# A chunked mLSTM encoder on one core: the forward state products move to other accumulator banks, and a token tile's norm joins the heads' norm

## The chip, the core and the metric

The kernel runs on one core of a Trainium2 chip. TensorE (PE in the profile) multiplies matrices into accumulator banks, VectorE (DVE) and ScalarE (ACT) work element by element and empty those banks, GpSimd (POOL) works on ordinary on-chip memory and issues some DMAs, SyncE (SP) issues most DMAs. Each engine goes through its own list of instructions in order and waits on semaphores for the others. The metric is the device time of one execution in microseconds (us).

## The reference, cut to what matters

The reference is one encoder layer on 2048 tokens of width 1024. It has an mLSTM mixer with four heads, run once forward and once backward over the tokens, a squared-ReLU MLP, and a gated embedding branch.

```python
def step(carry, xs):                       # one chunk of 128 tokens, all heads
    C, n, m = carry
    ...
    s = jnp.einsum('bhtd,bhsd->bhts', q_, k_) * d
    num = jnp.einsum('bhts,bhsv->bhtv', s, v_) + inter[..., None] * jnp.einsum('bhtd,bhvd->bhtv', q_, C)
    ...
    h = num / jnp.maximum(jnp.abs(den), jnp.exp(-m_t))[..., None]
    ...
    C = decay[..., None, None] * C + jnp.einsum('bhsv,bhsd->bhvd', w[..., None] * v_, k_)
...
h = (h_fwd + h_bwd)
h = h * lax.rsqrt(jnp.mean(jnp.square(h), axis=-1, keepdims=True) + EPS)     # the heads' norm
...
h = h + mix
h = h + sqrelu_mlp(rmsnorm(h, norm_mlp[i]), w1, w2)                          # the token norm
```

The two norms in this text are the heads' norm, one scale for each token and head, and the token norm ahead of the MLP, one scale for each token.

## The kernel before, in words

**Stages.** The kernel first projects the tokens to queries, keys, values and gates, and runs the backward states, from the start to 560 us. Then comes the chunk loop, to about 930 us, which is what the change touches. After it come the MLP's two matrix products and the gated branch, to the end. Every product in float32 precision is three matmuls of rounded parts (`mm3`, L185): high by high, high by low, low by high.

**Who sets the order.** The program writes the steps down by hand, as strings of step names (`ORDER`, L1519; `ORDER_1` and `ORDER_X`, L1564 and L1565). A scheduler of the framework then decides, from its own cost model and with the program's order as priority, in which order each engine issues its instructions and which buffer of a tag a tile gets. So the order on an engine can differ from the string. All engine calls outside the queues go through one helper, so nearly all rows of the profile have the line L100, and the tile names tell them apart.

**Accumulator banks.** There are three kinds (L65 to L72): four general banks (`ps_mm`), three for transposes (`ps_tr`) and one for scores (`ps_s`).

**A turn of the chunk loop** (L1566) works on chunk c. TensorE's part, by the tile that it writes: `pn` is the numerator of one direction (`nums`, L1006; step n0 forward, n1 backward), four general banks one after the other, each emptied by ScalarE's copy into `nt`. `pu` is the state product of a head (`state_update`, L781; step s): heads 0 and 1 take transpose banks, heads 2 and 3 general ones; VectorE's `Cn` reads it and forms the new state, which ScalarE rounds to `Chi` and VectorE subtracts to `Clo`. `pth` are the eight transposes of the finished heads of the chunk before (`transposes`, L1051; step T), in two transpose banks, read by VectorE's `og`; then ScalarE's `hThi` and VectorE's `hTlo`. `pS` are the scores of the next chunk (step S), whose masks come from ScalarE's exponentials `mb` (step e). `pso` are the two halves of the output projection of the chunk before (`out`, L1064; steps o0 and o1); VectorE's `xt` adds the input and SP stores the tile to `h1_d`.

**The heads' norm.** `norm` (L1026, step m) forms the denominators `rd` on VectorE, scales `nt`, and has ScalarE square each head into `jk` with the sum into a column of `ssh`. `norm_end` (L1045, step me) calls `rstd` (L169) on four columns: one VectorE operation (`rsa`), two on ScalarE (`rsy`), four small ones on VectorE (`rst`, `rsy`), and ScalarE scales the heads into `jk`.

**The token norm of the first half** (`Tokens0.steps`, L1155) is worked on in the chunk loop, since the tokens of early chunks are done by then. With XC = 6 (L1561), eight tiles are spread over turns 6 to 14: in turn c, `load` (xl) reads tile c - 6 into `raw`, and at the turn's end `norm` (xn) squares it on ScalarE with its sum in a column of its own (`ss1`), calls `rstd` on that one column and has VectorE scale it into `xs`. In turn c + 1, `tr` (xt) transposes it (`pt`, two transpose banks), ScalarE copies it into `zt`, and SP stores it.

**Buffers.** Tiles of 4 KB a partition share two tags: H with 39 buffers (L74) and O with 7 (L78). `raw`, `og`, `xt` and `zt` are of O.

Of the kernel before, what the change touches and what calls it, by code (L numbers as in the profile page):

```python
# [10 lines left out]
AF = mybir.ActivationFunctionType  # L11
ALU = mybir.AluOpType
# [4 lines left out]
P = 128  # L17
S = 2048
D = 1024
KD = D // P  # L20
NC = S // P
H = 4
# [3 lines left out]
DVX = DV + 2  # L26
# [9 lines left out]
def hybrid_mlstm_kernel(  # L36
# [20 lines left out]
    x, p, out = x[0], p[0, 0], out[0]  # L57
# [10 lines left out]
    def ps_tr(name):  # L68
        return psm.tile([P, 512], F32, tag="tr", bufs=3, name=name)
# [4 lines left out]
    def Ht(name, shape, dt=F32):  # L74

        return sb.tile(shape, dt, tag="H", bufs=NH, name=name)

    def Ot(name, shape, dt=F32):  # L78

        return sb.tile(shape, dt, tag="O", bufs=NO, name=name)  # L80
# [5 lines left out]
    class Engine:  # L86


        def __init__(self, engine):
            self.engine, self.last, self.strict = engine, None, False  # L90
# [18 lines left out]
    V, A, G, TE, SP = Engine(nc.vector), Engine(nc.scalar), nc.gpsimd, Engine(nc.tensor), nc.sync  # L109


    rowc = {}
# [10 lines left out]
    def act(o_, i_, func, **kw):  # L123
        name = "sigmoid" if func == AF.Sigmoid else "exp_ln"
        if name == "exp_ln" and table["set"] != name:
            in_order(lambda: A.preload_act_table_set("natural_log_exp_and_others"))
        table["set"] = name
        in_order(lambda: A.activation(o_, i_, func, **kw))
# [40 lines left out]
    def rstd(ss, n):  # L169

        T = lambda nm: sb.tile([P, 8], F32, tag=nm, bufs=3, name=nm)[:, :n]
        a, y, t = T("rsa"), T("rsy"), T("rst")
        V.tensor_scalar_add(a, ss, EPS)
        act(y, a, AF.Ln)
        act(y, y, AF.Exp, scale=-0.5)
        V.tensor_tensor(t, a, y, op=ALU.mult)
        V.tensor_tensor(t, t, y, op=ALU.mult)
        V.tensor_scalar(t, t, -0.5, 1.5, op0=ALU.mult, op1=ALU.add)
        V.tensor_tensor(y, y, t, op=ALU.mult)
        return y  # L180

    def small(nm, bufs=3):
        return sb.tile([P, 8], F32, tag=nm, bufs=bufs, name=nm)

    def mm3(ps, lh, ll, rh, rl, first, last, **kw):  # L185
        TE.matmul(ps, lh, rh, start=first, stop=False, **kw)
        TE.matmul(ps, lh, rl, start=False, stop=False, **kw)
        TE.matmul(ps, ll, rh, start=False, stop=last, **kw)
# [58 lines left out]
    class Prep:  # L247
# [16 lines left out]
        def square(self, j):  # L264
            if j == 0:
                self.ss, self.xs = small("ss"), []
            xs = Ht("xs", [P, D])
            A.activation(xs, self.raw[j], AF.Square, scale=1.0 / 32.0, accum_out=self.ss[:, j:j + 1])
            self.xs.append(xs)

        def norm(self):
            for j in range(4):
                self.square(j)
            self.scale()
# [55 lines left out]
        def steps(self):  # L330
            return [self.dma, self.norm] + [lambda k=k: self.tr(k) for k in range(KD)]
# [415 lines left out]
    def cols(t, d, c):  # L747

        return t.rearrange("p (d h c) -> p d h c", d=2, h=H)[:, d, :, c]
# [31 lines left out]
    def state_update(C, wk, vx, d, c):  # L781

        Cn = Ht("Cn", [P, H, DVX])
        for h in range(H):
            pu = (ps_tr if (h % 2 if d == 1 else h < 2) else ps_mm)("pu")[:, :DVX]
            mm3(pu, wk[:, 0, h], wk[:, 1, h], vx[0][:, h], vx[1][:, h], True, True)
            i = d * 64 + h * NC + c
            if C is None:
                V.tensor_copy(Cn[:, h, :], pu)
            else:  # L790
                V.scalar_tensor_tensor(Cn[:, h, :], C[:, h, :], dcb[:, i:i + 1], pu, op0=ALU.mult, op1=ALU.add)
        return Cn
# [140 lines left out]
    class Chunk:  # L933
        Cf = Cs = None

        def __init__(self, c):
            self.c = c

# [87 lines left out]
        def norm(self):  # L1026

            c, nt = self.c, self.nt
            rd = small("rd")
            for d in range(2):  # L1030
                den = nt[d][:, :, DV]
                r = rd[:, d * H:(d + 1) * H]
                V.scalar_tensor_tensor(r, den, -1.0, den, op0=ALU.mult, op1=ALU.max)
                V.tensor_tensor(r, r, cols(ecol, d, c), op=ALU.max)
            V.reciprocal(rd, rd)
            ss = small("ssh")
            jk = Ht("jk", [P, H, DV])
            for h in range(H):
                a, b = nt[0][:, h, 0:DV], nt[1][:, h, 0:DV]
                A.activation(a, a, AF.Copy, scale=rd[:, h:h + 1])  # L1040
                V.scalar_tensor_tensor(a, b, rd[:, H + h:H + h + 1], a, op0=ALU.mult, op1=ALU.add)
                A.activation(jk[:, h], a, AF.Square, scale=1.0 / 16.0, accum_out=ss[:, h:h + 1])
            self.ss, self.hr = ss, jk

        def norm_end(self):  # L1045
            rh = rstd(self.ss[:, :H], H)
            jk, nt = self.hr, self.nt
            for h in range(H):
                A.activation(jk[:, h], nt[0][:, h, 0:DV], AF.Copy, scale=rh[:, h:h + 1])
# [100 lines left out]
    class Tokens0(Right1):  # L1150
# [4 lines left out]
        def steps(self, t):  # L1155
            s = {}

            def load():
                s["raw"] = Ot("raw", [P, D])
                SP.dma_start(s["raw"], h1_d[t])  # L1160

            def norm():
                xs, ss = Ht("xs", [P, D]), small("ss1")
                A.activation(xs, s["raw"], AF.Square, scale=1.0 / 32.0, accum_out=ss[:, 0:1])
                r = rstd(ss[:, :1], 1)
                V.scalar_tensor_tensor(xs, s["raw"], r[:, 0:1], rowc["mlp"], op0=ALU.mult, op1=ALU.mult)
                s["xs"] = xs

            def tr():
                z = Ot("zt", [P, KD, P])  # L1170
                for g4 in range(2):
                    pt = ps_tr("pt")
                    for i in range(4):
                        k = g4 * 4 + i
                        TE.transpose(pt[:, i * P:(i + 1) * P], s["xs"][:, k * P:(k + 1) * P], ident)
                    A.copy(z[:, g4 * 4:g4 * 4 + 4], pt.rearrange("p (k t) -> p k t", t=P))
                sl = slice((t % 4) * P, (t % 4 + 1) * P)
                SP.dma_start(x0_d[t // 4, :, :, sl].rearrange("k p t -> p k t"), z)
            return [load, norm, tr]

        def zload(self, nm):
            j, l = int(nm[1]) - 1, int(nm[2]) - 1
# [235 lines left out]
    o, q = jobs[0, "o"], jobs[0, "q"]  # L1418
# [35 lines left out]
    p1 = pa[1][1]  # L1454
# [17 lines left out]
    for n, pr in ((0, pa[0][0]), (2, pa[0][1])):  # L1472
        e = pr.early()
# [40 lines left out]
    for at, f in zip(slots, steps[8:]):  # L1514
        at.append(f)
    assert len(slots) == len(steps) - 8

    ch = [Chunk(c) for c in range(NC)]
    ORDER = "n0 d1 s e T S p1 q n1 d2 k w sl m v d o0 o1 me".split()  # L1519

    def step(c, nm):
# [11 lines left out]
        if n2:  # L1533
# [7 lines left out]
    tr = {"o6a": o[6].groups[0], "o6b": o[6].groups[1], "o7a": o[7].groups[0], "o7b": o[7].groups[1], "D": z.dma, "D1": z.dma1, "p0": z.pre, "v0": z.split_v,  # L1541
          "e0": z.exps, "S0": z.scores, "k0": z.wk_split, "w0": z.weights, "q0": z.q_split,
          "d_": ch[1].dma, "p_": ch[1].pre}
# [12 lines left out]
    def row_load(nm, src):  # L1556
        rowc[nm] = Ht(f"row_{nm}", [P, D])
        SP.dma_start(rowc[nm], src.partition_broadcast(P))


    XC = 6  # L1561
    tp = {c: x0.steps(c - XC) for c in range(XC, XC + 8)}
    tp[XC][0] = lambda f=tp[XC][0]: (row_load("mlp", norm_mlp[0]), f())
    ORDER_1 = "n0 d1 s e T c6 S n1 d2 k w c7 q sl m v d o0 o1 me".split()  # L1564
    ORDER_X = "n0 d1 s e T S p1 q n1 xt d2 k xl w sl m v d o0 o1 me xn".split()  # L1565
    for c in range(1, NC - 1):  # L1566
        for nm in ORDER_X if c in tp or c - 1 in tp else ORDER if c > 1 else ORDER_1:
            if nm == "xt":

                tp.get(c - 1, [lambda: None] * 3)[2]()  # L1570
            elif nm in ("xl", "xn"):
                tp.get(c, [lambda: None] * 3)[("xl", "xn").index(nm)]()
            elif nm in ("c6", "c7"):
                wo[int(nm[1])].prep()
            else:
                step(c, nm)()
    TAIL = "d2 W n1 Z1 Z3 T n0 Z2 Z4 o0 m me P1 X1 o1 P2 T15 U3 U1 X2 U2 X3".split()
    l = ch[NC - 1]
# [34 lines left out]
    for i in range(2, NF // 2):  # L1613
        e0, e1 = ENTER[i - 1], ENTER[i]
        if i >= NF // 2 - 2:
            e0, e1 = (35, 38) if i == NF // 2 - 2 else (38, 40)
        down[max(e0 - 1, 0)].side.append(pairs[i].dma)
        steps = pairs[i].preps()
        for j, f in enumerate(steps):
            down[e0 + j * (e1 - e0) // len(steps)].side.append(f)  # L1620
# [73 lines left out]
```

## Time and profile before

| | us |
|---|---|
| median of 3 runs | 2441.32 |
| lowest and highest | 2438.54, 2443.88 |
| the profiled execution's own time | 2440.1 |
| its span, first to last instruction | 2438.4 |
| mean granted TensorE clock, of full speed | 0.995 |

The difference of 1.7 us between the execution's time and its span lies around the instructions. Rows of the profile give a start and a duration in us, the engine, the line, the operation, the tile written, the tiles read, the shape and the count. A bracket at the end of a row is the idle time of that engine just before the row and what ended it. A row of waits gives who waited for whom, the total in us, the number of times and the longest. The idle time of an engine that nobody waits for costs nothing.

The chunk loop in the trace: the first `pu` of chunks 1 to 14 starts at 579.00, 604.64, 626.38, 647.03, 668.40, 689.13, 710.46, 735.23, 760.07, 782.32, 807.26, 829.76, 855.53 and 877.08 us.

### The profile page before, as it was taken

To read this page: it belongs to the slowest core of one execution; us is meant where nothing else is said; L and a number is where in the kernel's file an instruction comes from. 1 tells how busy PE (TensorE), PEld (TensorE's weight loads), DVE (VectorE), ACT (ScalarE), POOL (GpSimd) and SP (SyncE) were. 2 spreads that over 40 slices of the span, in tenths; PEclk is the share of its full clock that TensorE was granted. 3 is DMA by queue.
4 is the path that set the end of the run, shared out by engine and by line. 5 is a ranking of instruction groups with operands and counts; after the bars stand their busy time and mean duration, and the time that the engine had idled before them with its cause. 6 is when DMAs were issued, how large, how long until landed. Compare 5 with 4: busy or idle time off the path is not lost.

```text
span 2438.4 us, 31719 instructions
## 1 busy us (share of the span) xinstructions
PE 2379.7 (98%) x11317; PEld 1962.4 (80%) x11317; DVE 1592.3 (65%) x2641; ACT 1168.6 (48%) x2182; POOL 606.3 (25%) x633
## 2 busy tenths in 40 slices
PE   7999999999999999999999999999999999999998
PEld 6978988788888887888888888787887888887776
DVE  6676555547788788566685544767666667656665
ACT  5234434437777774333353333544444444445554
POOL 1041121224333234446533332011111111110000
PEclk9999999999999999999999999999999999999999
DMA  5676656868767784456663332567677776893211
GB/s 174 225 227 193 187 159 220 297 204 296 243 208 246 242 274 133 132 158 189 234 229 104 109 109 71 169 140 172 158 184 166 181 165 153 187 227 93 79 56 48
DMA packets 264502, 429.11 MB, mean 176 GB/s; under 512 B 46952, under 2 KB 174312, under 8 KB 264344
## 3 DMA queue, kind: packets, MB, share of 16 engines
q1 hardware_dynamic: 204376, 303.23, 37.9%
q0 software_dynamic: 59680, 123.35, 21.3%
q8 instruction: 88, 1.44, 0.2%
q14 instruction: 70, 0.57, 0.1%
q10 hardware_dynamic: 288, 0.52, 0.1%
HBM read 257.62 MB, written 169.21 MB: 175 GB/s over the span
## 4 chain that ended last, share of the span: by engine, by line
PE 54%; DVE 4%; DMA 2%; ACT 2%; issue 1%; SPq 0%; POOL 0%; ACTq 0%; DVEq 0%; POOLq 0%
PE pa L100 28%; PE pb L100 14%; PE pc L100 7%; PE pg L100 4%; DMA hst<-hid_d 1%; PE pl L100 1%; ACT L100 1%; DVE h L100 1%; DVE xs L100 1%; PE pt L100 1%; DMA wst<-in_ple_w 1%; DVE op L100 1%; DVE rst L100 0%; DVE raw L100 0%; ACT g L100 0%
## 5 line engine op out<-in xcount | busy, mean ns | idle before, releaser
L100 PE MATMUL pa<-op 128*128 128x512 f32 x3360 | 824.7, 394 | 7.7 <-ACT e L100 4.0
L100 PEld LDWEIGHTS pa<-op 128*128 128x128 f32 x3360 | 629.6, 188 | 160.0 <-ACT e L100 6.9
L100 PE MATMUL pb<-op 128*128 128x512 f32 x1632 | 407.5, 394 | 0.9 <-DVE op L100 0.8
L100 PEld LDWEIGHTS pb<-op 128*128 128x128 f32 x1632 | 306.2, 188 | 73.5 <-DVE op L100 1.1
L100 DVE TENSOR_TENSOR op<-sa,op 128x1024 fp32r<-128x1024 f32 (+2 forms) x176 | 187.5, 1071 | 149.1 <-ACT op L100 113.9
L100 ACT CAST op<-sa 128x1024 fp32r<-128x1024 f32 (+2 forms) x176 | 156.3, 894 | 171.5 <-PE pb L100 84.3
L1284 POOL DMA_DIRECT2D h_d<-o x96 | 93.3, 974 | 561.1 <-DVE o L100 493.4
L100 ACT COPY e<-pa 128x512 f32<-128x512 f32 x160 | 93.8, 586 | 260.1 <-PE pa L100 259.3
L100 PE MATMUL pc<-op 128*128 128x512 f32 x768 | 192.0, 394 | 0.1
L100 PEld LDWEIGHTS pc<-op 128*128 128x128 f32 x768 | 144.1, 188 | 34.6 <-DVE op L100 0.5
L100 PE MATMUL psv<-whi,xT 128*128 128x272 f32 (+2 forms) x720 | 161.0, 317 | 0.6 <-DVE xT L98 0.6
L100 PE MATMUL psf<-xT,whi 128*128 128x512 f32 x512 | 160.6, 394 | 0.0
L100 DVE TENSOR_TENSOR op<-wst,op 128x512 fp32r<-128x512 f32 x112 | 124.3, 1112 | 35.6 <-ACT op L100 28.4
L100 ACT CAST op<-wst 128x512 fp32r<-128x512 f32 x112 | 92.5, 834 | 107.5 <-DVE op L100 59.5
L100 PEld LDWEIGHTS psv<-whi,xT 128*128 128x128 f32 x720 | 118.5, 188 | 9.9 <-DVE xT L98 0.8
L461 POOL TENSOR_TENSOR sa<-wst 128x512 f32<-128x512 f32 x32 | 58.8, 1838 | 263.6 <-PE pb L100 166.8
L100 PE MATMUL psv<-wlo,xT 128*128 128x272 f32 (+2 forms) x360 | 113.9, 316 | 0.0
L100 PEld LDWEIGHTS psf<-xT,whi 128*128 128x128 f32 x512 | 95.2, 188 | 21.4
L100 PE MATMUL pso<-whi,hThi 128*128 128x512 f32 x256 | 102.8, 402 | 4.8 <-ACT nt L100 3.5
L100 PE MATMUL pg<-whi,xTl 128*128 128x512 f32 x256 | 101.9, 398 | 0.0
L100 PE MATMUL pso<-wlo,hThi 128*128 128x512 f32 x256 | 101.4, 397 | 0.0
L100 PE MATMUL pso<-whi,hTlo 128*128 128x512 f32 x256 | 101.2, 396 | 0.0
(254 smaller groups left out, 4381.9 us busy)
## 6 DMA issues: line engine op xcount, KB each, us to landing
wst<-in_mlp_w SPq DMA_DIRECT2D x96, 512.0 KB
h_d<-o POOLq DMA_DIRECT2D x96, 512.0 KB, 12.3
hid_d<-e SPq DMA_DIRECT2D x128, 256.0 KB
hst<-hid_d SPq DMA_DIRECT2D x64, 384.0 KB
wst<-in_mlstm_w_in SPq DMA_DIRECT2D x44, 512.0 KB
vst<-v_d SPq DMA_DIRECT2D x31, 512.0 KB
raw<-in_x SPq DMA_DIRECT2D x16, 512.0 KB
kq<-kq_d SPq DMA_DIRECT2D x16, 512.0 KB
```

Source lines behind the costliest of these rows:

```text
L100: r = f(*a, **kw)
L461: eng.tensor_tensor(s[:, 0], r1[:, :, P:], r2[:, :, P:], op=add_)
L1284: G.dma_start(rows(h1_d, 2 * q + i), o[i], accum_op=add_)
```

## The change

Three edits, all in the chunk loop.

1. Forward state products (d == 0) take general banks for all four heads. The backward ones, which run before the loop, stay as they are.
2. The square of a token tile goes to a new step `xq`, between the exponentials and the head transposes of the turn, and puts its sum into a fifth column of that turn's `ssh`. `norm_end` then calls `rstd` on five columns, and the token norm is left with one VectorE operation (xn), which scales by the fifth column.
3. A token tile takes three turns: it is loaded in turn c, squared and scaled in turn c + 1, and transposed in turn c + 2. XC becomes 5, so that squares, scalings and transposes stay in the turns they were in, and the load comes a turn sooner. The tile that the square writes and the tile that the scaling writes are now two.

```diff
@@ state_update
-            pu = (ps_tr if (h % 2 if d == 1 else h < 2) else ps_mm)("pu")[:, :DVX]
+            pu = (ps_tr if d == 1 and h % 2 else ps_mm)("pu")[:, :DVX]
@@ class Chunk
+        ss, nss = None, H
+
@@ Chunk.norm
-            ss = small("ssh")
+            ss = self.ss = self.ss or small("ssh")
...
-            self.ss, self.hr = ss, jk
+            self.hr = jk
@@ Chunk.norm_end
-            rh = rstd(self.ss[:, :H], H)
+            rh = self.rh = rstd(self.ss[:, :self.nss], self.nss)
@@ Tokens0.steps
-            def norm():
-                xs, ss = Ht("xs", [P, D]), small("ss1")
-                A.activation(xs, s["raw"], AF.Square, scale=1.0 / 32.0, accum_out=ss[:, 0:1])
-                r = rstd(ss[:, :1], 1)
-                V.scalar_tensor_tensor(xs, s["raw"], r[:, 0:1], rowc["mlp"], op0=ALU.mult, op1=ALU.mult)
-                s["xs"] = xs
+            def square(chunk):
+                chunk.ss, chunk.nss = small("ssh"), H + 1
+                A.activation(Ht("xs", [P, D]), s["raw"], AF.Square, scale=1.0 / 32.0, accum_out=chunk.ss[:, H:H + 1])
+
+            def norm(chunk):
+                s["xs"] = Ht("xs", [P, D])
+                V.scalar_tensor_tensor(s["xs"], s["raw"], chunk.rh[:, H:H + 1], rowc["mlp"], op0=ALU.mult, op1=ALU.mult)
...
-            return [load, norm, tr]
+            return [load, square, norm, tr]
@@ the loop
-    XC = 6
+    XC = 5
-    ORDER_X = "n0 d1 s e T S p1 q n1 xt d2 k xl w sl m v d o0 o1 me xn".split()
+    ORDER_X = "n0 d1 s e xq T S p1 q n1 xt d2 k xl w sl m v d o0 o1 me xn".split()
     for c in range(1, NC - 1):
-        for nm in ORDER_X if c in tp or c - 1 in tp else ORDER if c > 1 else ORDER_1:
-            if nm == "xt":
-
-                tp.get(c - 1, [lambda: None] * 3)[2]()
-            elif nm in ("xl", "xn"):
-                tp.get(c, [lambda: None] * 3)[("xl", "xn").index(nm)]()
+        for nm in ORDER_X if {c, c - 1, c - 2} & set(tp) else ORDER if c > 1 else ORDER_1:
+            if nm == "xl" and c in tp:
+                tp[c][0]()
+            elif nm == "xq" and c - 1 in tp:
+                tp[c - 1][1](ch[c])
+            elif nm == "xn" and c - 1 in tp:
+                tp[c - 1][2](ch[c])
+            elif nm == "xt" and c - 2 in tp:
+                tp[c - 2][3]()
             elif nm in ("c6", "c7"):
                 wo[int(nm[1])].prep()
-            else:
+            elif nm[0] != "x":
                 step(c, nm)()
```

## The prediction

> **What bounds the kernel now.** The page comes first: TensorE is busy for nearly the whole span, so time can come only from stretches in which it waits or runs slowly.
>
> ```profile
> PE 2379.7 (98%) x11317; PEld 1962.4 (80%) x11317; DVE 1592.3 (65%) x2641; ACT 1168.6 (48%) x2182; POOL 606.3 (25%) x633
> ```
>
> The change touches only the chunk loop. Its place in time is given by the tiles `pn` and `pu` (the heads' numerators and the state products), which run from 559 to 901 us. So the next view is TensorE's own waits in 580 to 900 us:
>
> ```profile
> PE pth L100 <- DVE Cn L100: 14.6, 11, 3.0
> PE pso L100 <- ACT nt L100: 3.5, 5, 2.0
> PE pu L100 <- ACT nt L100: 0.7, 1, 0.7
> PE pn L100 <- DVE xt L100: 0.4, 1, 0.4
> ```
>
> One wait is three quarters of the total: the head transposes `pth` wait eleven times for VectorE's state update `Cn`. `pth` has no use for `Cn`; the link is a bank. Two of the three transpose banks hold `pu` of heads 0 and 1 until `Cn` has read them, and the second group of `pth` needs one of the two.
>
> What a turn costs with and without that wait is read from the busy table cut at each first `pu` of chunks 7 to 14 (columns: us; busy us of PE, PEld, DVE, ACT, POOL with counts; granted clock, DMA share, GB/s):
>
> ```profile
> 710.46:735.23 24.77, 22.76 (x135) 20.40 (x133) 19.22 (x42) 18.97 (x52) 7.86 (x11) 0.93 0.70 244
> 735.23:760.07 24.84, 22.78 (x134) 20.45 (x133) 19.67 (x41) 18.58 (x51) 8.91 (x11) 0.93 0.70 245
> 760.07:782.32 22.25, 21.47 (x135) 18.94 (x133) 18.38 (x41) 19.22 (x54) 7.12 (x11) 1.00 0.76 261
> 782.32:807.26 24.94, 22.77 (x134) 20.40 (x133) 19.43 (x41) 18.68 (x51) 7.61 (x11) 0.93 0.68 233
> 807.26:829.76 22.50, 21.22 (x134) 18.86 (x133) 18.96 (x44) 18.34 (x52) 7.11 (x11) 1.00 0.77 257
> 829.76:855.53 25.77, 22.74 (x135) 20.38 (x133) 20.41 (x41) 18.98 (x52) 8.44 (x12) 0.93 0.66 225
> 855.53:877.08 21.55, 21.16 (x134) 18.83 (x133) 18.45 (x38) 18.46 (x52) 7.94 (x11) 1.00 0.78 269
> ```
>
> The last turn is nearly clean: 21.16 us of TensorE work. The seven take 166.62 us where 7 x 21.16 = 148.1, so 18.5 us lie above the floor. They split in two. In the four long turns TensorE is also busy for 1.6 us more with the same matmuls, at a clock of 0.93 (together 6.4 us); the rest is waiting. Two waits show the size from which the clock falls:
>
> ```profile
> 739.56 1.11 PE L100 MATMUL pth<-ident,jk 128*128 128x128 f32 x4 [2.06 <-DVE Cn L100]
> 810.60 0.66 PE L100 MATMUL pth<-ident,jk 128*128 128x128 f32 x4 [1.28 <-DVE Cn L100]
> ```
>
> After 2.06 us the turn is at 0.93, after 1.28 us at 1.00. [...]
>
> **Why `Cn` is late.** VectorE's timeline before the second of those waits:
>
> ```profile
> 731.11 0.15 DVE L100 TENSOR_SCALAR rsa<-ss 128x1 f32<-128x1 f32 x1
> 732.53 0.69 DVE L100 TENSOR_TENSOR xt<-pso,xt 128x512 f32<-128x512 f32 x1 [1.27 <-PE pso L100]
> 733.78 0.85 DVE L100 TENSOR_TENSOR rst<-rsa,rsy 128x1 f32<-128x1 f32 x1 [0.56 <-ACT rsy L100]
> 734.66 1.21 DVE L100 TENSOR_TENSOR rst<-rst,rsy 128x1 f32<-128x1 f32 x1
> 735.91 0.15 DVE L100 TENSOR_SCALAR rst<-rst 128x1 f32<-128x1 f32 x1
> 736.10 0.16 DVE L100 TENSOR_TENSOR rsy<-rsy,rst 128x1 f32<-128x1 f32 x1
> 736.29 1.72 DVE L100 SCALAR_TENSOR_TENSOR xs<-raw,rsy,row_mlp 128x1024 f32<-128x1024 f32 x1
> 737.94 0.59 DVE L100 SCALAR_TENSOR_TENSOR rd<-nt 128x4 f32<-128x4 f32 x1
> 738.56 0.55 DVE L100 TENSOR_TENSOR rd<-rd,ecol 128x4 f32<-128x4 f32 x1
> 739.03 1.65 DVE L100 SCALAR_TENSOR_TENSOR Cn<-Cn,dcb,pu 128x258 f32<-128x258 f32 x4
> ```
>
> The token tile's own norm chain holds VectorE from the end of `xt` (733.22) to 736.29, that is 3.07 us of small operations and a wait for ScalarE; then `xs` follows with 1.72. The last `pu` had been issued long before:
>
> ```profile
> 736.55 0.28 PE L100 MATMUL pu<-vh,wk 128*128 128x258 f32 x1
> 735.56 0.36 ACT L100 COPY nt<-pn 128x257 f32<-128x257 f32 x1
> 740.72 1.05 ACT L100 CAST Chi<-Cn 128x1032 fp32r<-128x1032 f32 x1 [3.33 <-DVE Cn L100]
> 729.51 1.04 ACT L100 ACTIVATE xs<-raw 128x1024 f32<-128x1024 f32 x1
> ```
>
> **The change part by part.**
>
> *Fifth column.* Eight chains of five small VectorE operations and two ScalarE ones (the `rsy` pair) go; the heads' chain does the same operations on 128x5 instead of 128x4. A 128x1 row costs 0.15, the wider one, in the heads' chain, this:
>
> ```profile
> 728.36 0.17 DVE L100 TENSOR_SCALAR rsa<-ssh 128x4 f32<-128x4 f32 x1
> ```
>
> so the added column costs nothing that can be seen. `xs` becomes ready when the heads' chain ends, at about 731.2 (the token's chain starts at 731.11 only behind it), in the 1.27 us in which VectorE waits for `pso`. If it is issued there, 0.2 to 0.4 us of it stick out and `xt` ends near 733.6; if after `xt`, it ends near 734.9. In both cases VectorE is free before the numerators are copied (735.92), and `Cn` can start at about 736.4 (after two `rd` of about 0.2) in place of 739.03: 2.6 us earlier, and with it 0.4 us before `pu` ends. If the `rd` keep their 1.1 us it is 1.8 us earlier.
>
> *Three turns.* The load of a token tile moves one turn ahead, to the same place in its turn, so no queue sees a new order within a turn: on SP it stays behind the store of `zt` and the load of `xt` and ahead of the next chunk's loads, and POOL issues nothing new. The tile stays in its buffer a turn longer, one more of seven in use; a load delayed by that would be for the next turn's use, 20 us later, so I take zero. The square (1.04, with its accumulator read about 1.1) leaves the stretch before the heads' scaling, where ScalarE waits for VectorE anyway, and lands behind the exponentials, where ScalarE now stands idle for 3.33 us. When `Cn` comes 2.6 us earlier that gap is 0.7 us, so the square can push `Chi` and all behind it back by up to 0.4 us. The chain from `Chi` to the copies that free the next `pso` bank is at the edge already in the third turn of the table, so this is one term of the allowance below:
>
> ```profile
> 768.22 0.50 PE L100 MATMUL pso<-whi,hThi 128*128 128x512 f32 x1 [0.52 <-ACT nt L100]
> ```
>
> *General banks.* `pth` no longer meets `pu`. But heads 0 and 1 of `pu` now need the banks that the copies `nt` free, and all four `pn` of the second direction need `Cn`. The second is cheap. Between `pu` and `pn` lie eight `pth` and the scores, 1.7 us where nothing waits, as in chunk 3:
>
> ```profile
> 627.83 1.04 PE L100 MATMUL pth<-ident,jk 128*128 128x128 f32 x8
> 629.51 0.37 PE L100 MATMUL pn<-vh,pTh 128*128 128x258 f32 x1
> ```
>
> In the turn shown `pn` would so come at 738.4, and `Cn` of head 0, done at 739.5 before, is done by 737.7 even at 1.8 us earlier. The first is dearer. Here are the copies and the first `pu` of chunk 4, where no token norm runs and the exponentials stand between the copies:
>
> ```profile
> 647.03 0.28 PE L100 MATMUL pu<-vh,wk 128*128 128x258 f32 x1
> 648.03 0.36 ACT L100 COPY nt<-pn 128x257 f32<-128x257 f32 x1
> 648.59 0.36 ACT L100 COPY nt<-pn 128x257 f32<-128x257 f32 x1
> ```
>
> With 0.36 us a head, head 3 of `pu` would start at 648.1 and can't before 649.0: 0.9 us of new wait. With the copies as in the turn of 735.56 it would be zero (head 3 at 736.3, copy done at 735.92). Both ends hold for the turns with norms as well, since their ScalarE will now be as close behind TensorE as in chunk 4. I take 0.45 us a turn, midway, the square's push included; a wait of that size leaves the clock alone by the rows above.
>
> **The sum.** Chunks 7 to 13: 18.5 - 7 x 0.45 = 15.3 us won. Of the 14.6 us of waits for `Cn` the seven turns hold 11.2:
>
> ```profile
> L100 PE MATMUL pth<-ident,jk 128*128 128x128 f32 x56 | 9.4, 294 | 11.2 <-DVE Cn L100 11.2
> ```
>
> The other 3.4 us go too, against 0.45 us in each of chunks 2 to 6 and 14 (2.7 us): +0.7. In chunks 0 and 1 there is no such wait to win, and `pn` of the second direction follows `pu` at once in chunk 0:
>
> ```profile
> 562.17 0.28 PE L100 MATMUL pn<-vh,pTh 128*128 128x258 f32 x1
> 562.32 1.42 DVE L100 COPY Cn<-pu 128x258 f32<-128x258 f32 x4
> 579.00 0.28 PE L100 MATMUL pu<-vh,wk 128*128 128x258 f32 x1
> 580.58 1.15 ACT L100 COPY nt<-pn 128x257 f32<-128x257 f32 x4
> ```
>
> The first `Cn` copy ends near 562.7, so `pn` loses 0.6 us, and `pu` some 0.3 before it. In chunk 1 the copies come in one block at 580.58, 1.6 us behind the first `pu`; most of that is in the 0.7 us of `pu` and the longest wait of `pso`, 2.0 us, both of which TensorE waits there already. I charge 1.5 us for both. Sum: 15.3 + 0.7 - 1.5 = 14.5 us. What follows the loop is TensorE at work throughout, so the gain reaches the end whole. The profiled execution took 2440.1 us (span 2438.4 and 1.7 around it), 1.2 us under the median of 2441.3; 14.5 off the median is 2426.8.
>
> With the allowance at 0 the gain is 14.5 + 13 x 0.45 = 20; at 0.95 it is 8.
>
> **The rivals.**
>
> *Slower: the bank wait on the copies.* If ScalarE's order puts the exponentials ahead of the numerators' copies in every norm turn, `pu` waits as chunk 1's would: 2 us, at which the clock falls, 3.6 us a turn. Eight turns (7 to 14) cost 29; less the 20 recovered, 9 us slower: about 2450. It decides once the copies end more than 2 us behind the numerators. Against it: in the norm turns they end 0.5 us behind. [...] 8 in 100.
>
> *Half: `Cn` stays late.* If VectorE's order keeps `xs` and the `rd` in front of `Cn` and finds no gap for them, only the 1.7 us of work between `pu` and the second `pn` are won in each turn. Of the four long waits about 1 us each remains (739.5 against 738.4 in the turn shown), and the clock is saved: 18.5 - 4 - 7 x 0.45 - 1.5 for chunks 0 and 1 = 9.9, and less where the remainder is larger, so about 9 us, 2432. 18 in 100.
>
> *Nothing: ScalarE takes over.* ScalarE is busy 18.5 us of a clean turn and now has an order with fewer gaps. If its chain from the copies to the scaled heads takes 24 us a turn whatever VectorE does, the turns keep their length: within 4.9 us of 2441. Against it: the last turn of the table holds the same ScalarE work in 21.55 us. 8 in 100.
>
> *All of it: the whole 20 us or a little more*, 2419 to 2421. 8 in 100. The forecast itself (2423 to 2430) gets 58.
>
> **Numbers.** 2426.8 is the likeliest case. 2418 to 2437 takes in the allowance from 0 to 0.95 and the half case. A change of 0.2% (4.9 us) is about what a measurement can tell here. Faster 0.84, same 0.08, slower 0.08.
>
> **What would show it.** Right: no `pth` waits for `Cn`; turns of 21.2 to 22.1 us at clock 1.00 from chunk 7 to 13; `Cn` starts within 0.5 us of the last `pu`; new short waits of `pu` for `nt`. Wrong: a wait of 2 us or more in any turn, `pn` waiting for `Cn`, ScalarE without a gap and `pso` waiting for `nt`, or turns over 23 us.

## The result and the profile after

The changed kernel takes 2425.41 us (median of 4 runs, 2423.09 to 2428.63) against 2441.24 us for the kernel before on the same chip: the ratio is 0.9939, with a 95% interval of 0.9927 to 0.9951. The medians differ by 15.8 us; 14.5 was forecast. The profiled execution took 2426.04 us (span 2424.3).

The waits of TensorE in 580 to 900 us in the profile after (who waited for whom, us in total, times, longest):

```profile
PE pso L100 <- ACT nt L100: 2.5, 2, 1.4
PE pu L100 <- ACT nt L100: 1.8, 5, 0.7
PE pn L100 <- DVE Cn L100: 1.4, 1, 1.4
PE pn L100 <- DVE vl L100: 1.2, 1, 1.2
```

The line that had headed this view, `pth` for `Cn` with 14.6 us, is gone, and no line of its size has come in its place. The busy table cut at each first `pu` of chunks 6 to 14 (columns as before: us; busy us of PE, PEld, DVE, ACT, POOL; granted clock, DMA share, GB/s):

```profile
693.11:715.61 22.50, 21.13 (x127) 18.28 (x125) 16.63 (x35) 17.41 (x49) 6.39 (x11) 1.00 0.59 184
715.61:736.91 21.30, 21.30 (x134) 18.97 (x133) 16.89 (x35) 18.11 (x50) 7.48 (x10) 1.00 0.84 279
736.91:757.91 21.00, 21.00 (x135) 18.86 (x133) 16.91 (x35) 18.00 (x50) 7.50 (x10) 1.00 0.86 289
757.91:778.89 20.98, 20.98 (x135) 18.85 (x133) 16.96 (x35) 18.03 (x50) 7.50 (x10) 1.00 0.86 280
...
841.90:862.89 20.99, 20.99 (x134) 18.86 (x133) 16.94 (x35) 18.03 (x50) 9.41 (x10) 1.00 0.78 254
```

In turns 7 to 13 (all rows but the first; those left out are 21.00 and 21.01) the length of a turn and TensorE's busy time are the same number: nothing waits, and the clock is 1.00 throughout. Together they take 147.28 us where they took 166.62, 19.3 us less. VectorE is busy for 16.9 us a turn where it was 18.4 to 20.4. VectorE in the turn of 736.91, from the heads' chain on:

```profile
733.40 0.17 DVE L100 TENSOR_TENSOR rsy<-rsy,rst 128x5 f32<-128x5 f32 x1
733.60 1.28 DVE L100 SCALAR_TENSOR_TENSOR xs<-raw,rsy,row_mlp 128x1024 f32<-128x1024 f32 x1
734.80 0.68 DVE L100 TENSOR_TENSOR xt<-pso,xt 128x512 f32<-128x512 f32 x1
737.55 0.88 DVE L100 SCALAR_TENSOR_TENSOR Cn<-Cn,dcb,pu 128x258 f32<-128x258 f32 x2 [2.06 <-PE pu L100]
```

`Cn` starts 0.64 us after the first `pu` (736.91); it was 3.8 us before (739.03 against 735.23). The bracket says that VectorE now waits 2.06 us for TensorE: the direction of the wait has turned round.

Three places give something back. From the first `pu` of chunk 0 to that of chunk 1 it takes 20.28 us (before 18.27), turn 6 takes 22.50 (before 21.33), and the profiled execution reached the loop 2.85 us later than that of before (563.58 against 560.73). The instructions up to there are the same and stand in the same order, but for two of VectorE's clearing operations that changed places with one `vl`, and over all traces of this case the loop begins anywhere between 560.7 and 564.3 us. So that is a difference between executions and not between the kernels.

One of the prediction's signs of being wrong is there once: `pn` waits 1.4 us for `Cn`, in chunk 1 (587.67) and in no turn with a token norm.

### The profile page after: what moved, and what is told of

It reads as the page before. It is cut to its first block, busy times and chain, and to the rows that moved or that the text cites. A ratio compares the mean times of both kernels' runs of the same rounds, so it can differ in the third digit from the quotient of the medians.

```text
span 2424.3 us, 31650 instructions
## 1 busy us (share of the span) xinstructions
PE 2375.9 (98%) x11317; PEld 1958.0 (81%) x11317; DVE 1573.3 (65%) x2601; ACT 1163.7 (48%) x2166; POOL 601.8 (25%) x633
## 4 chain that ended last, share of the span: by engine, by line
PE 77%; issue 8%; DVE 6%; DMA 4%; ACT 4%; POOL 1%; SPq 0%; DVEq 0%; ACTq 0%; POOLq 0%
PE pa L100 30%; PE pb L100 15%; PE pc L100 7%; PE psf L100 6%; PE pso L100 5%; PE pg L100 4%; PE psv L100 4%; PE pn L100 3%; PE pu L100 1%; PE pt L100 1%; PE pl L100 1%; ACT L100 1%; DMA hst<-hid_d 1%; DMA cb_d<-Clo 1%; DVE h L100 1%
## 5 line engine op out<-in xcount | busy, mean ns | idle before, releaser
L100 PE MATMUL pg<-whi,xTh 128*128 128x512 f32 x256 | 101.1, 395 | 0.0
L100 PE MATMUL pg<-wlo,xTh 128*128 128x512 f32 x256 | 101.0, 394 | 0.0
```

Source lines behind the costliest of these rows:

```text
L100: r = f(*a, **kw)
```

## The experiments

Two theories stood at the start. The first is the prediction's: `Cn` comes early because the token's chain of small operations is folded into the heads' chain (fifth column), and the general banks take `pth` off `Cn` altogether. The rival: one edit does it all, and the others are worth nothing. A third theory came up on the way, from the durations of VectorE's rows. The runs were taken on several chips, so each ratio is to the kernel before on the same chip (medians of 2438.2 to 2441.4 us).

### The banks alone

The kernel before with only the `pu` line of the change.

```diff
-            pu = (ps_tr if (h % 2 if d == 1 else h < 2) else ps_mm)("pu")[:, :DVX]
+            pu = (ps_tr if d == 1 and h % 2 else ps_mm)("pu")[:, :DVX]
```

> Only the bank edit: all four forward state products in general banks; the token norm as before (own chain, two turns). Theory 1 (the late VectorE chain is the cause, the bank only carries it to TensorE): the state update Cn stays as late as before in chunks 7 to 14, the eight head transposes no longer wait, and the numerators of the second direction wait for Cn instead, about 1 us in the four turns that had 2 us or more; those turns lose their clock penalty. Time 2430 to 2434, some 9 us won, turns of 22 to 23 us. Theory 2 (the shared transpose bank is the cause): the waits are gone and nothing takes their place, 2424 to 2427, turns of 21 us.

Measured: 2439.12 us, ratio 0.9992 (0.9981 to 1.0004). TensorE's first two waits in the loop (580 to 900 us, here and below):

```profile
PE pn L100 <- DVE Cn L100: 8.5, 8, 1.9
PE pso L100 <- ACT nt L100: 5.4, 8, 1.4
```

`pth` is free, and the waits moved on. `pn` of the second direction needs the new state itself, so it stands for `Cn`; and as `Cn` is late, `Chi` and ScalarE's copies of the numerators behind it are late too, so `pso` stands for the banks that these empty. Turns 7 to 13 take 164.2 us, 2.4 less than before; over the whole time the interval takes in no change at all.

### The norm and the turns alone

The change with the old `pu` line.

> Only the norm edit: fifth column, early square, three turns; the state products of heads 0 and 1 stay in the transpose banks. Theory 1 (late VectorE chain): Cn starts within 0.5 us of the last state product, the head transposes wait at most 0.3 us a turn in chunks 7 to 14, the waits in chunks 2 to 6 stay (2.2 us together) and the 2 us that the changed kernel loses in chunks 0 and 1 come back: 2423 to 2427, as fast as the whole change. Theory 2 (the shared bank): waits of the transposes for Cn of 1 us or more a turn stay, 2431 to 2438.

Measured: 2425.37 us, ratio 0.9935 (0.9923 to 0.9947), the whole gain. Turns 7 to 13 take 146.8 us. The step from chunk 0 to 1 is back at 18.27 us: the 2.0 us lost there belong to the general banks.

### Old banks in chunks 0 and 1

```diff
-            pu = (ps_tr if d == 1 and h % 2 else ps_mm)("pu")[:, :DVX]
+            pu = (ps_tr if (h % 2 if d == 1 else h < 2 and c < 2) else ps_mm)("pu")[:, :DVX]
```

> The whole change, but in chunks 0 and 1 heads 0 and 1 take transpose banks as before. If the 2 us that chunks 0 and 1 take longer after the change come from the general banks there (state products waiting for the numerators' copies, numerators waiting for Cn), they come back: 1 to 2.5 us under the changed kernel, 2423 to 2424.5, and the first state product of chunk 1 follows that of chunk 0 after 18.3 us, not 20.3. Rival (they come from the run, as the 2.9 us before chunk 0 do): no difference from the changed kernel, 2425.5.

Measured: 2426.08 us, ratio 0.9941 (0.9926 to 0.9956). In the trace the first step is 18.27 us, but the next is 26.2 where the change has 25.5. The 1.3 us won in the sum can't be seen in the median.

### The early square with a chain of its own

The change, but the square puts its sum into a column of its own and the token has its own `rstd`; load, square and turns as in the change.

```diff
-                chunk.ss, chunk.nss = small("ssh"), H + 1
-                A.activation(Ht("xs", [P, D]), s["raw"], AF.Square, scale=1.0 / 32.0, accum_out=chunk.ss[:, H:H + 1])
+                s["ss"] = small("ss1")
+                A.activation(Ht("xs", [P, D]), s["raw"], AF.Square, scale=1.0 / 32.0, accum_out=s["ss"][:, 0:1])
...
-                V.scalar_tensor_tensor(s["xs"], s["raw"], chunk.rh[:, H:H + 1], rowc["mlp"], op0=ALU.mult, op1=ALU.mult)
+                r = rstd(s["ss"][:, :1], 1)
+                V.scalar_tensor_tensor(s["xs"], s["raw"], r[:, 0:1], rowc["mlp"], op0=ALU.mult, op1=ALU.mult)
```

> The whole change without the fifth column: the square still comes early in the turn and the tile takes three turns, but its sum goes to a column of its own and the token norm has its own chain of five small VectorE and two ScalarE operations again. Theory A (what counts is that the square is done before the heads' chain starts, so that VectorE can run both chains side by side): as fast as the whole change within 2 us, 2424 to 2428, Cn within 0.5 us of the last state product, 0.6 to 1 us more small VectorE work a turn. Theory B (what counts is that the chain's seven operations are gone): Cn comes 2 to 3 us later again in chunks 7 to 14, 2430 to 2434.

Measured: 2424.87 us, ratio 0.9938 (0.9925 to 0.9951). The eight chains are all still there and cost nothing: VectorE runs the two chains in step, so the fifth column is not what wins.

### The three turns alone

The same with the old banks: of the change only the order of load, square and transposes is left.

> Three turns and the early square alone: old banks, and the token norm with its own column and its own chain. Theory A (the early square alone is the gain): as fast as the whole change within 2 us, 2423 to 2428, turns of 21 us, Cn within 0.7 us of the last state product. Rival (two of the three edits together are needed, and each single run before kept one of the other two): 2430 to 2440.

Measured: 2425.90 us, ratio 0.9951 (0.9937 to 0.9964); turns 7 to 13 take 147.1 us. A row of VectorE, where x2 counts one operation of each chain:

```profile
730.70 0.23 DVE L100 TENSOR_TENSOR rst<-rsa,rsy 128x4 f32<-128x4 f32 x2
```

The interval takes in the ratio of the whole change, 0.9939. So one edit carries the gain, with the other two undone. It has two halves: the load comes a turn earlier, and the square moves in front of the heads' norm.

### The fifth column with the load in the same turn

The change with two turns: `XC = 6`, and the square behind the load of its own turn.

```diff
-    XC = 5
+    XC = 6
...
-    ORDER_X = "n0 d1 s e xq T S p1 q n1 xt d2 k xl w sl m v d o0 o1 me xn".split()
+    ORDER_X = "n0 d1 s e T S p1 q n1 xt d2 k xl w sl xq m v d o0 o1 me xn".split()
...
```

> The whole change with two turns for a token tile instead of three: loaded and squared in the same turn (the square ahead of the heads' squares), scaled at its end, transposed in the next; fifth column and general banks as in the change. Theory A (the square must be done before the heads' chain starts, so that nothing of the token norm stands between that chain and the state update): the column brings that about here too, so Cn stays within 0.7 us of the last state product and the time within 3 us of the whole change, 2424 to 2428; ScalarE has the square in its busier half, which costs at most 0.4 us in each of eight turns. Rival (the third turn is what counts: the tile's load comes too late for a square in the same turn, and the heads' chain now waits for it): the heads' chain starts 1 to 3 us later, head transposes or the next chunk's copies are late, turns of 22 to 24 us, 2432 to 2445.

Measured: 2441.24 us, ratio 1.0007 (0.9997 to 1.0016). ScalarE's waits in 700 to 900 us, and one of them in its timeline:

```profile
ACT jk L100 <- DVE rsy L100: 21.0, 9, 3.5
ACT xs L100 <- DMA raw<-h_d: 17.0, 7, 3.5
```

```profile
797.65 1.06 ACT L100 ACTIVATE xs<-raw 128x1024 f32<-128x1024 f32 x1 [3.44 <-DMA raw<-h_d]
```

Without the third turn the square has to wait for its load (17.0 us in seven turns), and in the shared chain it holds the heads' norm back with it (21.0 us of `jk` waiting, 14.1 in the change). Turns 7 to 13 take 163.7 us: the fold and the banks without the third turn give nothing that shows in the time.

### The load early, the square late

The other half by itself: three turns, but square and chain at the end of the turn, as before; own column, old banks.

```diff
...
-    ORDER_X = "n0 d1 s e xq T S p1 q n1 xt d2 k xl w sl m v d o0 o1 me xn".split()
+    ORDER_X = "n0 d1 s e T S p1 q n1 xt d2 k xl w sl m v d o0 o1 me xq xn".split()
```

> The token tile is loaded a turn ahead (three turns), but its square and its own norm chain stay at the end of the turn, behind the heads' norm, as in the kernel before; old banks, own column. If the gain is that the square stands ahead of the heads' norm, so that its chain no longer follows the heads' chain in front of Cn (order theory): 2436 to 2443, eleven or so waits of pth for Cn, 12 to 16 us in all, turns 7 to 13 between 22 and 26 us. If the gain is that the square no longer waits for its load (load theory): 2424 to 2430, no wait of pth over 1 us.

Measured: 2438.89 us, ratio 0.9999 (0.9990 to 1.0009), with `pth` for `Cn` at 13.5 us in eleven waits. An early load is worth nothing by itself. The early square without it ran only with the fifth column (the run above), and gave nothing either, so both halves are needed as far as the runs go. VectorE and GpSimd in one of its turns:

```profile
732.78 0.99 DVE L100 TENSOR_TENSOR rst<-rsa,rsy 128x1 f32<-128x1 f32 x1 [0.48 <-ACT rsy L100]
733.80 1.21 DVE L100 TENSOR_TENSOR rst<-rst,rsy 128x1 f32<-128x1 f32 x1
```

```profile
732.46 2.54 POOL L978 TENSOR_TENSOR ib<-kq,ib 128x512 f32<-128x512 f32 x2 [10.44 <-DMA ib<-in_d]
```

Two operations on one column take 0.99 and 1.21 us, where the same operations in the heads' chain take 0.16. GpSimd's two products `ib` run at that time, 1.29 us each; the first ends at 733.75 and the second at 734.99, and VectorE's two operations end at 733.76 and 735.01. The kernel before shows the same. Over the norms of turns 6 to 13, from VectorE's `rst` and `xs` (ns: shortest, median, longest), and then GpSimd beside the rows from 733.78 to 739.03 that the prediction shows:

```profile
L100 DVE TENSOR_TENSOR rst<-rst,rsy x16: 159/162/1294, 706.6 to 876.6; 128x4 f32<-128x4 f32 x8, 128x1 f32<-128x1 f32 x8
L100 DVE TENSOR_SCALAR rst<-rst x16: 153/162/170, 706.8 to 877.9; 128x4 f32<-128x4 f32 x8, 128x1 f32<-128x1 f32 x8
L100 DVE SCALAR_TENSOR_TENSOR xs<-raw,rsy,row_mlp x8: 1284/1426/2281, 711.2 to 878.3; 128x1024 f32<-128x1024 f32 x8
```

```profile
733.32 2.53 POOL L976 TENSOR_TENSOR ib<-kq,ib 128x512 f32<-128x512 f32 x2 [11.92 <-PE pn L100]
...
736.93 2.15 POOL L986 TENSOR_SCALAR_AFFINE_SELECT mb<-mb 128x512 f32<-128x512 f32 x2
```

The operation with one tile as its input (`TENSOR_SCALAR`) takes 0.17 at the longest, and a `rsa` of this kind took 0.14 in the middle of an `ib` (at 758.01; that `ib` ran from 757.63 to 758.92). Those with two tiles take up to 1.29, and `xs` up to 2.28. In the turn shown the excess is 0.69 + 1.05 us on `rst`, beside `ib`, and 0.84 on the two `rd`, which end 0.02 us after the two selections `mb` (738.52 and 739.11 against 738.50 and 739.09). `xs` is 0.44 longer there too, but in the turn of 782.32 an `xs` beside a selection took 1.29, so what lengthened this one isn't shown. Together it is 3.0 us in front of `Cn`, of which 2.6 end with an operation of GpSimd. So a third theory: the chain is late not because it is long, but because it runs beside GpSimd's work.

### GpSimd's product moved, nothing else

The kernel before; in the turns with token tiles three one-column GpSimd operations, which add zero, tie `ib` to a place behind the selections `mb`, where the changed kernel has it too in turns 7 to 13 (not in turn 14).

```diff
+            if late:
+                z = small("zlate")
+                G.tensor_tensor(z[:, 0:1], self.mb[:, 1, 0, 0:1], self.mb[:, 1, 0, 0:1], op=ALU.subtract)
+                for d in range(2):
+                    G.tensor_tensor(self.ib[:, d, 0, 0:1], self.ib[:, d, 0, 0:1], z[:, 0:1], op=ALU.add)
             for d in range(2):
                 G.tensor_tensor(self.ib[:, d], self.kq[:, 1], self.ib[:, d], op=ALU.mult)
...
+            elif nm == "p1" and (c in tp or c - 1 in tp):
+                ch[c + 1].pre(late=True)
```

> The kernel before, with one thing moved: in the turns with token tiles GpSimd's product ib of the next chunk comes behind its selections mb (three one-column GpSimd operations, which add zero, tie it there). In the trace of before the token chain's rst operations take 0.80 to 1.29 us in place of 0.16, and end as an ib product ends, so VectorE stands still behind GpSimd. Blocking theory: with ib out of the way the chain is some 2 us shorter in each turn, Cn comes within about 1 us of the first pu, and the time is 2424 to 2431; rst 0.16 us each. Order theory (a chain of five small operations, a ScalarE round trip and xs behind the heads' chain is late by itself): rst 0.16 us, but pth still waits 1 us or more for Cn in most turns, 2434 to 2441.

Measured: 2429.79 us, ratio 0.9953 (0.9937 to 0.9969). TensorE's first two waits in the loop, VectorE in the turn that was looked at before, and GpSimd:

```profile
PE pso L100 <- ACT nt L100: 7.6, 10, 2.0
PE pth L100 <- DVE Cn L100: 2.4, 5, 0.7
```

```profile
732.83 0.16 DVE L100 TENSOR_TENSOR rst<-rsa,rsy 128x1 f32<-128x1 f32 x1 [1.07 <-ACT rsy L100]
733.03 0.16 DVE L100 TENSOR_TENSOR rst<-rst,rsy 128x1 f32<-128x1 f32 x1
...
733.61 1.28 DVE L100 SCALAR_TENSOR_TENSOR xs<-raw,rsy,row_mlp 128x1024 f32<-128x1024 f32 x1
...
735.43 1.65 DVE L100 SCALAR_TENSOR_TENSOR Cn<-Cn,dcb,pu 128x258 f32<-128x258 f32 x4
```

```profile
737.29 2.56 POOL L981 TENSOR_TENSOR ib<-kq,ib 128x512 f32<-128x512 f32 x2
```

The chain is where it was, with its own ScalarE round trip and with `xs` behind it, and `Cn` still comes in time: 1.66 us after the first `pu` (733.77), where it was 3.8, and the waits of `pth` fall from 14.6 to 2.4 us. Turns 7 to 13 take 153.9 us: 12.7 of the 19.3 us. Of the 6.6 us left, 3.3 are `pso` waiting for the copies `nt`, about 1 us in each of three turns; the remainder was not traced to a cause. So, by the trace, the larger part of what the change won is time that VectorE's operations had lost beside GpSimd's `ib` (the two `rst` take 0.16 us each here, where they took 0.85 and 1.21), and no part of the change aimed at that.

### The norm behind the state update, in two turns and in three

If the place ahead of `Cn` is what hurts, the whole token norm can also go behind it. Own chain, old banks; first with two turns:

```diff
...
-    XC = 5
+    XC = 6
...
-    ORDER_X = "n0 d1 s e xq T S p1 q n1 xt d2 k xl w sl m v d o0 o1 me xn".split()
+    ORDER_X = "n0 d1 s e xq xn T S p1 q n1 xt d2 k xl w sl m v d o0 o1 me".split()
...
```

> A token tile keeps two turns and its own norm chain, old banks, but square, chain and scaling stand behind the state update of the next turn: Cn comes ahead of them on VectorE. Order theory: all that matters is that Cn is not behind the chain, so 2424 to 2431, Cn within 1 us of the first pu, turns of 21 to 21.8 us. Rival, the chain costs wherever it stands once it is on the path of a turn (here in front of hTlo, and on ScalarE, waiting for rsa, in front of hThi): 2433 to 2445, pso waits for hTlo or for nt by 1 us or more a turn.

Measured: 2448.86 us, ratio 1.0039 (1.0025 to 1.0053). `Cn` comes 0.6 to 1.7 us behind the first `pu`, and yet the loop is no shorter. TensorE's first waits in it:

```profile
PE pt L100 <- DVE xs L100: 12.7, 8, 2.0
PE pso L100 <- ACT nt L100: 6.5, 11, 2.0
PE pth L100 <- DVE Cn L100: 2.3, 4, 0.8
```

The transposes `pt` of the same turn now wait for the late `xs`. (Of the 9.5 us between this profiled execution and that of before only 2.2 lie in the loop up to chunk 14; the rest lies behind it and was not traced to a cause.) The same order with `XC = 5` and the transposes a turn later:

> As the run with the norm behind the state update, but with three turns: load in turn c, square, own chain and scaling behind the update in turn c + 1, transposes in turn c + 2. If that run lost its gain only because the transposes of the same turn wait for the late xs (12.7 us in eight waits), a turn more between xs and pt gives it back: 2423 to 2429, no wait of pt, Cn within 1 us of the first pu, turns of 21 to 21.5 us. If the chain costs by standing in front of hTlo and rd on VectorE, and by rsy in front of hThi on ScalarE: 2430 to 2440, pso waiting for hTlo or nt by 0.5 us or more a turn.

Measured: 2450.29 us, ratio 1.0043 (1.0029 to 1.0056). Turns 7 to 13 take 167.0 us, as long as before. No `pt` waits any more, but TensorE's waits are now headed by `pso`, and ScalarE shows why:

```profile
PE pso L100 <- ACT nt L100: 18.5, 12, 2.0
```

```profile
766.50 1.05 ACT L100 CAST Chi<-Cn 128x1032 fp32r<-128x1032 f32 x1 [1.03 <-DVE Cn L100]
767.46 1.06 ACT L100 ACTIVATE xs<-raw 128x1024 f32<-128x1024 f32 x1
769.03 0.20 ACT L100 ACTIVATE rsy<-rsa 128x1 f32<-128x1 f32 x1 [0.42 <-DVE rsa L100]
...
770.90 0.59 ACT L100 COPY zt<-pt 128x512 f32<-128x512 f32 x1 [0.41 <-PE pt L100]
...
772.81 1.21 ACT L100 COPY nt<-pn 128x257 f32<-128x257 f32 x4
```

From `Chi` to the copies it is 6.31 us here. In the run with the three turns alone it is 4.00 (758.13 to 762.13): there the `rsy` pair is not in this stretch, and the order puts `zt` behind the copies. Of the 2.3 us more, 0.9 are the pair and its wait for `rsa`, and 1.4 are `zt` and a wait for `pt`. They come back as 1.95 us of `pso` in every turn. So it is not enough to take the chain away from `Cn`: between `Chi` and the copies ScalarE is on TensorE's path, and what is put there costs nearly as much as it takes.

### A late VectorE, with old banks and with new

Do the general banks at least make the kernel more patient of a late `Cn`? Both kernels have the new norm and turns, and VectorE gets five extra passes behind `xs` (four over `xs`, one over the decay tile that `Cn` reads), which leave the values as they are.

```diff
+                for _ in range(4):
+                    V.scalar_tensor_tensor(s["xs"], s["xs"], 1.0, s["xs"], op0=ALU.mult, op1=ALU.max)
+                V.scalar_tensor_tensor(dcb, s["xs"][:, :P], 0.0, dcb, op0=ALU.mult, op1=ALU.add)
```

> The norm edit with the old banks, and VectorE made late on purpose: in each of the eight turns with a token norm, four more passes over the scaled tile (1.3 us each, values unchanged) and a pass over the decay table that reads them stand ahead of the state update Cn, so that it comes about 3 us later. Theory 1 (VectorE's lateness ahead of Cn is the whole cause): most of the gain goes, 2434 to 2444, turns of 23 to 25 us. Rival (the gain came from the place of ScalarE's square, and VectorE has room to spare): turns stay under 22 us, 2425 to 2430.

> The same four passes ahead of the state update Cn, with general banks for all four state products (the whole change otherwise). Theory 1: the late Cn costs nearly as much here, since the numerators of the second direction and ScalarE's rounding of the state wait for it instead of the head transposes: 2432 to 2444, turns of 22.5 to 24.5 us, within 4 us of the run with the old banks. Rival (general banks make TensorE independent of a late Cn): 2425 to 2430.

Measured: 2472.87 us with the old banks (ratio 1.0147, 1.0133 to 1.0160) and 2473.98 with the new (1.0144, 1.0128 to 1.0160). TensorE's first two waits in the loop, old banks and then new:

```profile
PE pso L100 <- ACT nt L100: 22.1, 12, 3.5
PE pth L100 <- DVE Cn L100: 5.5, 5, 2.2
```

```profile
PE pso L100 <- ACT nt L100: 19.4, 9, 2.4
PE pn L100 <- DVE Cn L100: 7.3, 8, 1.0
```

The cost is the same with both, and larger than either theory had it. Part of that is the size of the delay: with the new banks `Cn` starts 5.4 to 6.1 us after the first `pu`, where the change has 0.6, so it is 4.8 us later and more, not 3. Its turns take 27.3 us on the mean, and in each of turns 7 to 13 the clock falls once (granted clock of the profiled execution 0.993, where the change has 0.997). A late `Cn` delays ScalarE's `Chi`, and through it the copies that free the banks of `pso`, whichever bank `pu` sits in.

## Why the prediction was right, step by step

**The bound** was right: the waits of `pth` for `Cn` and the clock that fell with them were what could be won, in turns 7 to 13, and nothing took their place.

**Why `Cn` is late** was right as to which rows lie in front of it and wrong as to why they are slow. Of the "3.07 us of small operations and a wait for ScalarE", 1.74 us are what two `rst` took over 0.16 us each beside GpSimd's `ib`, and 0.84 of the 1.1 us of `rd` is such an excess beside its selections. The quoted rows held the clue, 0.85 and 1.21 us for operations on one column beside rows of 0.15 and 0.16 for the same shape; no row of GpSimd stands beside them.

**The fifth column** was credited with removing the eight chains. They do go, but the run with a chain of its own shows that they cost nothing once the square is early. What the prediction said of the place was right: `xs` comes right behind the heads' chain, in VectorE's wait for `pso`; `xt` ends 1.4 us before the first `pu` (735.48 against 736.91; 1.6 in the first of its two cases), and `Cn` starts 0.6 us before the last `pu` ends (0.4 was forecast).

**The three turns** were costed at zero, as a condition for the fold. Zero cost is right, but they are the edit that gives the gain: the load a turn earlier lets the square stand before the heads' norm, so that the token's chain runs in step with the heads' chain, with no GpSimd product beside its small operations. Two things changed at once there, the chain's place and that of `ib`, which the scheduler moved behind the selections in turns 7 to 13. Moving `ib` alone gives two thirds. What the chain's place gives with `ib` left where it was can be seen in turn 14 alone, where both products still start ahead of the first `pu`. In the run with the three turns alone (`Cn` and `xs` of VectorE, then GpSimd; the first `pu` at 860.73):

```profile
857.59 2.42 DVE L100 SCALAR_TENSOR_TENSOR xs<-raw,rsy,row_mlp 128x1024 f32<-128x1024 f32 x1
861.28 1.67 DVE L100 SCALAR_TENSOR_TENSOR Cn<-Cn,dcb,pu 128x258 f32<-128x258 f32 x4 [0.67 <-PE pu L100]
857.63 3.54 POOL L978 TENSOR_TENSOR ib<-kq,ib 128x512 f32<-128x512 f32 x2 [8.79 <-DMA ib<-in_d]
```

Beside `ib`, `xs` takes 2.42 us in place of 1.28, and `Cn` still starts 0.55 us after the first `pu`. So in that turn the early chain was enough by itself; no run had it so in all turns.

The square landed behind `Chi` and not ahead of it, so it does not delay `Chi`; it delays the copies, which shows in turn 6 alone, where there is no `pt` between `pn` and `pso`: 1.1 us of `pso` for `nt`.

**The general banks** were given an allowance of 0.45 us in each of 13 turns. In turns 7 to 13 it is 0: this is the term that was sized wrongly, by 3.2 us (7 x 0.45). The other 0.8 us there come from turns of 21.0 us, not 21.16. The 1.5 us charged to chunks 0 and 1 were 2.0 in the first step, and turn 6 costs 1.2, where the allowance was 0.45. The edit as such is worth nothing in either direction that can be measured (0.9992 alone; 0.9939 with it and 0.9935 without).

**The sum** came out by errors that offset each other. Between the first `pu` of chunk 0 and that of chunk 14 the trace gains 17.0 us: 19.3 in turns 7 to 13 and 0.9 in turns 1 to 5, less 2.0 in the first step and 1.2 in turn 6. The profiled execution gave 2.85 of it up ahead of the loop; the medians differ by 15.8. The forecast had the right waits and the right place of `Cn`, and it gave the credit to the wrong edits. As all three were in the change, the time didn't show that; in this the number was luck.

**The rivals.** *Half*, `Cn` late with the new banks, was priced at 9 us from "the 1.7 us of work between `pu` and the second `pn`". The banks alone are that case, and gave 2 us by the median, an amount that the interval doesn't set apart from nothing. The price left 4 us of waiting for `Cn`; in turns 7 to 13 of that run `pn` waits 8.1 us for it. It also left out that a late `Cn` makes `Chi` and the copies late: `pso` waits 3.5 us for `nt` in these turns, where it was 0.5. *Slower* and *nothing* did not come; the longest wait of `pu` is 0.7 us. What *nothing* feared is seen with another order, if in another stretch of ScalarE's work: with the norm behind the update the way from `Chi` to the copies does set the turns.

## What to carry to other kernels

When an engine's small operation takes five times its usual time, look at what the neighbour engine is doing at that moment before moving the operation: here moving one GpSimd product was worth two thirds of a change that rewrote three things. The bank that "someone else holds" was here only the first place where a late result shows; ask who is next to need the late result before pricing its release. Of a change with several edits, run each alone: a step that was meant as preparation may be the one that pays.

## What the runs showed of the hardware

**VectorE beside GpSimd.** In turns 6 to 13 of the kernel before, VectorE's `rst` operations with two tiles as inputs took 0.16 us at the median. Ten of 32 took 0.80 to 1.29, and each of these ended 0.01 or 0.02 us after one of GpSimd's products `ib`, which took 1.28 to 1.31 us each. The `TENSOR_SCALAR` operations of the two chains, with a single tile, took 0.14 to 0.17 us, one of them in the middle of an `ib`.

**A wait of some 2 us and the clock.** The prediction took it that the clock falls at a wait of 2 us, from a turn with 2.06 us at 0.93 and one with 1.28 us at 1.00. In the run with the early load and the late square the same turn holds a wait of 2.06 us of `pth`, at a clock of 1.00:

```profile
734.28:757.51 23.23, 21.17 (x134) 18.88 (x133) 20.16 (x41) 18.34 (x52) 8.60 (x11) 1.00 0.75 261
```

In the run with three turns and the norm behind the update each of seven turns holds a `pso` wait of 1.94 or 1.95 us, and three of them fall, at a price of 1.5 us of TensorE's time:

```profile
787.35:810.58 23.23, 21.28 (x134) 18.89 (x133) 16.96 (x40) 18.58 (x53) 7.62 (x11) 1.00 0.75 252
810.58:835.33 24.75, 22.80 (x134) 20.06 (x133) 17.00 (x40) 18.85 (x53) 7.78 (x11) 0.93 0.73 233
```

The traces' own records of the clock show each of the five falls in the loop of before as 3.41 us at half the clock; they begin at 589.41, 715.71, 739.60, 787.38 and 835.17 us, the last four in the four long turns. Cut into stretches of that length, with borders at the falls, the loops of before and after (560 to 905 us, 100 stretches each) hold five stretches with 2.01 to 3.03 us idle, all of them before the change, and each is followed by a fall. The others hold 1.43 us or less, and none is followed by one. Here are two pairs of neighbouring stretches in the run with three turns and the norm behind the update, cut in the same way (us; TensorE's busy us; clock, DMA share, GB/s), each with a wait of 1.95 us in the first or across the border:

```profile
745.17:748.58 3.41, 1.46 (x14) 1.00 0.45 184
748.58:752.00 3.42, 3.42 (x8) 0.50 0.84 210
792.96:796.37 3.41, 1.54 (x14) 1.00 0.38 151
796.37:799.78 3.41, 3.33 (x14) 1.00 0.80 203
```

With the wait whole in one stretch (1.95 us idle) the next runs at half the clock; with 1.87 in it and 0.08 in the next the clock stays at 1.00. In the run with the banks alone one fall, at 717.7 us, comes after 1.20 us of idle time by the profile. So in these runs a wait of some 2 us came with a fall and without one, and what decides between the two was not shown. In the kernel before each of the four long turns has its fall, and the prediction was right to count the 6.4 us.
